# Second pass of the scores on 128 rows: keys' hi and lo parts in two copies each, in a two-layer hybrid encoder

## Chip, cores and metric

One core of a Trainium2 chip runs the whole program as one launch. The metric is the device time of one execution in microseconds (us); the median over runs is compared. The profile is of one execution, whose own time is given beside its span.

## What is computed

The reference is a two-layer encoder on 512 tokens of width 1024. Each layer projects the normalised residual stream once and feeds four token mixers in parallel:

- A: latent attention of 4 heads over all 512 keys, with a contraction of 64 + 32 = 96;
- B: attention in a band of +-128 tokens, 4 query heads of 64 on 2 key heads, with a sink per head;
- C: neighbourhood attention on an 8 x 64 grid, 4 heads of 64;
- D: three groups of dilated band attention, 4 heads of 64 each, combined by their softmax denominators.

Each mixer's output is projected, multiplied by a sigmoid gate and summed; an output projection, a LayerNorm, a squared-ReLU MLP with a gated embedding and a second LayerNorm follow. For a head of 64 the scores are

```python
s = jnp.einsum('bnqhgd,bnkhd->bnhgqk', qb, kw).astype(jnp.float32) * dh ** -0.5
```

so the contraction of a score is over 64 values only.

## The kernel before

**Numbers in two parts.** Matmul operands are split into a hi part (rounded to fp32r by an ACT copy, `acopy`, L106) and a lo part (the rest, by a DVE subtraction, `vsub`, L109). A product of two matrices is hi x hi + hi x lo + lo x hi, three passes into the same PSUM bank. For weights the 128x1024 chunk is loaded by a DMA on SP's queue (`load`, L149), its hi part is made by ACT (L106) and its lo part by POOL (L170); a GEMM tile (`gemm_T`) takes 24 matmuls of 128x512.

**Heads of 64.** The array has 128 rows and a head needs 64. `evac_q2` puts one head's hi part into 64 partitions of a slot and its lo part into the other 64, for two heads a slot each. `evac_k2` (L353) takes the PSUM tile of two key heads and makes three slots: `ka` with the hi part of the first head in both halves, `kb` with that of the second head in both halves, and `kl` with the lo part of the first head in the upper half and of the second in the lower. ACT makes two copies of 64x512 and DVE two subtractions, both from PSUM; then L365 and L366 copy each hi part to the other half, from SBUF to SBUF on DVE. `QK.scores` (L378) then needs two matmuls for a score tile: the first over all 128 rows (q hi and q lo times k hi), the second over 64 rows (q hi times k lo):

```python
P.mm(out, qv(self.q), kv(self.k), True, False)
P.mm(out, qv(self.qh), kv(self.kl), False, True)
```

`evac_k2` is called five times a layer: for B (tile `T` 2), for C (7 and 8) and for D (12 and 18). `QK.scores` is called 16 times a layer in each of B, C (in `attn_band`) and D (in `attn_D`, where four matmuls of `FD` over 64 rows follow it directly).

**Order of the work.** The program is in written order on each engine. `Prog.run` interleaves a list of main generators (GEMM tiles, cut into granules of `P.gran` matmuls) with a list of small steps (`pipeline`, L444): each step of an attention issues the scores and softmax of one unit (S), the scaling of an earlier one (N), its transposes (T) and the product with the values (V), with lags of 1, 3 and 5 steps in A and B, and 1, 5 and 7 in C and D. So TensorE gets blocks of main matmuls with attention matmuls between them. The run of stage A ends with the three tiles of B's queries and keys; the run of stage B begins with 8 matmuls of its first main tile and then the first scores of B.

**The arena.** `R` holds `N_SLOT` slots of 128x512, 16 of them the normalised stream. `Arena.alloc` takes the next run of free slots after the last one given, in a ring; `release` frees. A weight chunk takes 4 slots. `Prog.ahead` decides how far weights are split ahead of their use: up to two chunks beyond the one taken (`P.look`), one more if many slots are free, and none that isn't needed at once while free slots less 4 are below `P.least` (7 from the start of a layer to the end of its stage D, then 0).

Of the kernel before, what the change touches and what calls it, by code (L numbers as in the profile page):

```python
# [11 lines left out]
F32 = mybir.dt.float32  # L12
# [5 lines left out]
DEPTH = 2  # L18
ALPHA = float((2 * DEPTH) ** 0.25)
NEG = -1e30  # L20
N_SLOT = 64


class Arena:
    def __init__(self, n):
        self.free = [True] * n
        self.at = 0
# [18 lines left out]
class Prog:  # L46
    def __init__(self, ctx, tc, a, out):
# [13 lines left out]
        self.PS = ps.tile([128, 8, 512], F32, name="PS")  # L61
        self.R = const.tile([128, N_SLOT, 512], F32R, name="R")
        self.M = const.tile([128, 8, 512], F32, name="M")
# [11 lines left out]
        self.hh, self.hl = 0, 8  # L75
        self.ar = Arena(N_SLOT)
        for i in range(16):
# [272 lines left out]
    return sa, sb  # L350


def evac_k2(P, ps, src=None):  # L353
    nc = P.nc
    sa, sb, sl = P.ar.alloc(1), P.ar.alloc(1), P.ar.alloc(1)
    ka, kb, kl = P.R[:, sa, :], P.R[:, sb, :], P.R[:, sl, :]
    v = lambda x: x
    if src:
        ps = src(ps)
        v = lambda x: x.rearrange("p (c t) -> p c t", c=4)  # L360
    P.acopy(v(ka)[0:64], ps[0:64])
    P.acopy(v(kb)[64:128], ps[64:128])
    P.vsub(v(kl)[0:64], ps[0:64], v(ka)[0:64])
    P.vsub(v(kl)[64:128], ps[64:128], v(kb)[64:128])
    nc.vector.tensor_copy(ka[64:128], ka[0:64].bitcast(F32))  # L365
    nc.vector.tensor_copy(kb[0:64], kb[64:128].bitcast(F32))  # L366
    return sa, sb, sl


class QK:  # L370


    def __init__(self, P, q, k, kl, pos):
        self.q, self.k = P.R[:, q, :], P.R[:, k, :]
        r = slice(0, 64) if pos == 0 else slice(64, 128)
        self.qh, self.kl = P.R[r, q, :], P.R[r, kl, :]

    def scores(self, P, out, qv, kv):  # L378
        P.mm(out, qv(self.q), kv(self.k), True, False)
        P.mm(out, qv(self.qh), kv(self.kl), False, True)  # L380

# [363 lines left out]
def layer(P, l, pend):  # L747

    nc, a = P.nc, P.a
    tok = lambda c: (lambda k: P.R[:, P.hh + k, 128 * c:128 * c + 128], lambda k: P.R[:, P.hl + k, 128 * c:128 * c + 128])  # L750
    P.gb = [0, 1, 2]
    P.least, P.reserve = 7, 24


    P.look, P.extra, P.more = 0, 0, 6
# [67 lines left out]
    kv, kvw = [], []  # L823
# [117 lines left out]
    def a_end():  # L941
# [3 lines left out]
    B = {}  # L945
    P.gran = GRAN['A']
    tB = [T_tile(0, store(B, 0, lambda ps: evac_q2(P, ps, 0.125))),
          T_tile(1, store(B, 1, lambda ps: evac_q2(P, ps, 0.125))),
          T_tile(2, store(B, 'k', lambda ps: evac_k2(P, ps)))]
    steps_A = [a_first, a_second]  # L950
    for h in range(4):
# [33 lines left out]
    D = {'qk': {}}  # L985
# [39 lines left out]
    yA = Y(P)  # L1025
    P.run([gateA(j) for j in range(8)] + tB, steps_A + pre(lambda: biasB(0)) + attn_A(P, A, yA))
    qb = {0: (B[0][0], 0), 2: (B[0][1], 1), 1: (B[1][0], 0), 3: (B[1][1], 1)}
    headB = [QK(P, qb[h][0], B['k'][h // 2], B['k'][2], qb[h][1]) for h in range(4)]


    brw = {}
# [18 lines left out]
    def vC(i):  # L1050
        def evac(ps):
# [18 lines left out]
          T_tile(5, store(C, 'q0', lambda ps: evac_q2(P, ps, 0.125)), True),  # L1070
          T_tile(6, store(C, 'q1', lambda ps: evac_q2(P, ps, 0.125)), True),
          T_tile(7, store(C, 'k0', lambda ps: evac_k2(P, ps)), True),
          T_tile(8, store(C, 'k1', lambda ps: evac_k2(P, ps)), True)]
    yB = Y(P)
    stB = attn_band(P, 'B', headB, lambda h, j: vBt[:, j, h // 2].rearrange("p x d -> p (x d)"), biasB, yB,
# [13 lines left out]
    headC = []  # L1089
    for h in range(4):  # L1090
        q, k = C[f'q{h // 2}'], C[f'k{h // 2}']
        headC.append(QK(P, q[h % 2], k[h % 2], k[2], h % 2))


    def gated(n, j, y, last=False):
# [49 lines left out]

    def d_heads(p, t):
        for i in range(2):
            D['qk'][2 * p + i] = QK(P, t['q'][i], t['k'][i], t['k'][2], i)

    def d_free(t):  # L1150
        for s in [*t['q'], *t['k']]:
# [7 lines left out]
    vD_far()  # L1159
    P.run(near0 + far0)  # L1160
    d_heads(0, t0)
    P.run([gated(2, j, yC) for j in range(4)] + near1, attn_D(P, D, (0, 1), yD) + pre(lambda: bias_first(2)))
    d_free(t0)
    P.run(far1)
    d_heads(1, t1)
    P.run([gated(2, j, yC) for j in range(4, 8)], attn_D(P, D, (2, 3), yD))
    d_free(t1)
# [114 lines left out]
    for gi, (j0, j1) in enumerate(FF_GROUPS):  # L1282
        fs = []
        for j in range(j0, j1):
            w = P.take((l, 'f1', j))
            ps = P.PS[:, P.bank(), :]
# [3 lines left out]
            r = P.tmp("relu")  # L1290
# [3 lines left out]
            s = P.ar.alloc(1), P.ar.alloc(1)  # L1294
# [26 lines left out]
    for c in range(4):  # L1321
        ps = P.PS[:, P.bank(), :]
# [24 lines left out]
def hybrid_encoder(ctx: ExitStack, tc: tile.TileContext, a, out):  # L1347
# [3 lines left out]
    with tc.manual_schedule():  # L1351
# [33 lines left out]
        for l in range(DEPTH):  # L1385
            pend = layer(P, l, pend)
# [117 lines left out]
```

## Time and profile before

| | us |
|---|---|
| median of 3 runs | 1997.35 (1996.52 to 1997.78) |
| the profiled execution's own time | 1997.37 |
| its span, first to last instruction | 1995.5 |
| TensorE (PE) busy | 1954.3 |
| POOL, DVE, ACT busy | 840.3, 777.1, 755.2 |

The page gives busy time by engine, the chain of work that ended last, and groups of instructions by line. Most instructions come from helpers, so matmuls all have line L94 (transposes L97), ACT copies L106 and DVE subtractions L109; the shapes tell them apart. A matmul's row reads `rows*columns` of the weights, then `rows x columns` of the moving data. Matmul records overlap: the end of one is modelled, so the pace of TensorE is read from start to start. A weight load (PEld) is a record of its own.

### The profile page before, as it was taken

The page shows a single profiled execution, that of the slowest core. Times are in us where ns is not written, and L with a number is a line of the kernel's source. Part 1 is how long each engine was busy: PE and PEld are TensorE (multiplying, and loading weights), DVE is VectorE, ACT ScalarE, POOL GpSimd, SP SyncE. Part 2 cuts the span into 40 slices and gives each one's busy share as a digit, 9 for nine tenths or more (in the row PEclk, how much of TensorE's full clock was granted, in tenths as well). Part 3 has the DMA queues.
Part 4 walks back from the last instruction along what each step waited for, and adds up shares of the span by engine and source line. Part 5 has one row for each costly group of instructions (what it writes and reads, how often), then busy time and mean ns, then how long its engine had stood idle before and what let it go on. Part 6 is the DMA issues. An engine that isn't in the chain of part 4 may idle for free.

```text
span 1995.5 us, 24072 instructions
## 1 busy us (share of the span) xinstructions
PE 1954.3 (98%) x9440; PEld 1611.4 (81%) x9440; DVE 777.1 (39%) x1565; ACT 755.2 (38%) x1313; POOL 840.3 (42%) x407
## 2 busy tenths in 40 slices
PE   7999999999999999999999999999999999999998
PEld 6777878787888888888888788787888888888886
DVE  6665564435243202112366656625332621021125
ACT  4554544434324322313235544434333333133130
POOL 4322344433655453534532224343436545345352
PEclk9999999999999999999999999999999999999999
DMA  4312232221432232323332123232314233223232
GB/s 168 108 54 82 99 112 97 89 82 61 147 117 95 96 126 74 107 87 103 122 111 68 57 82 103 82 125 72 101 56 168 96 102 101 102 84 127 67 120 78
DMA packets 59697, 195.96 MB, mean 98 GB/s; under 512 B 6720, under 2 KB 11968, under 8 KB 59584
## 3 DMA queue, kind: packets, MB, share of 16 engines
q1 hardware_dynamic: 56256, 188.13, 28.0%
q0 software_dynamic: 1152, 4.19, 0.7%
q10 hardware_dynamic: 2176, 2.10, 0.3%
q8 instruction: 74, 1.21, 0.2%
q14 instruction: 39, 0.32, 0.1%
HBM read 186.01 MB, written 8.39 MB: 97 GB/s over the span
## 4 chain that ended last, share of the span: by engine, by line
PE 66%; DVE 3%; ACT 1%; POOL 1%; DMA 1%; issue 1%; DVEq 0%; ACTq 0%; POOLq 0%
PE PS L94 64%; PE PS L97 2%; ACT R L106 1%; POOL R L170 1%; DVE R L109 1%; DMA raw<-in_wO_dram 0%; DMA raw<-in_wPL_dram 0%; DVE gate L1254 0%; DVE FD L303 0%; DVE FD L301 0%; DVE p L394 0%; ACT p L386 0%; DVE qf L916 0%; DVE ysum L421 0%; DVE rt L915 0%
## 5 line engine op out<-in xcount | busy, mean ns | idle before, releaser
L94 PE MATMUL PS<-R 128*128 128x512 f32 (+4 forms) x8528 | 1886.2, 378 | 12.3 <-DVE R L365 5.3
L94 PEld LDWEIGHTS PS<-R 128*128 128x128 f32 (+1 forms) x8528 | 1508.5, 187 | 333.0 <-issue 37.6
L170 POOL TENSOR_TENSOR R<-raw,R 128x1024 fp32r<-128x1024 f32 (+1 forms) x304 | 734.7, 2421 | 848.5 <-ACT R L106 811.2
L106 ACT ACTIVATE R<-raw 128x1024 fp32r<-128x1024 f32 x306 | 321.1, 1053 | 340.8 <-PE PS L94 143.5
L106 ACT ACTIVATE R<-PS 128x128 fp32r<-128x128 f32 (+5 forms) x300 | 131.7, 450 | 131.9 <-PE PS L97 82.3
L109 DVE TENSOR_TENSOR R<-PS,R 128x512 fp32r<-128x512 f32 (+5 forms) x276 | 134.4, 494 | 118.7 <-ACT R L106 117.5
L1109 POOL TENSOR_TENSOR M<-M,gate 128x512 f32<-128x512 f32 x48 | 62.1, 1293 | 191.7 <-DVE gate L1108 135.5
L386 ACT ACTIVATE p<-p,s 128x256 f32<-128x256 f32 (+2 forms) x96 | 66.1, 688 | 187.1 <-DVE s L551 65.4
L1293 DVE TENSOR_TENSOR ff<-relu 128x512 f32<-128x512 f32 x64 | 44.3, 692 | 222.1 <-ACT relu L1291 222.1
L1305 DVE TENSOR_TENSOR FD<-FD,PS 128x512 f32<-128x512 f32 x40 | 27.5, 687 | 242.5 <-PE PS L94 242.5
L1291 ACT ACTIVATE relu<-PS 128x512 f32<-128x512 f32 x64 | 38.3, 599 | 168.5 <-PE PS L94 168.5
L394 DVE TENSOR_SCALAR p<-p,s 128x512 f32<-128x512 f32 (+3 forms) x128 | 95.0, 742 | 4.5
L97 PE MATMUL PS<-ident,p 128*128 128x128 f32 x480 | 73.6, 273 | 2.8 <-DVE p L394 1.7
L97 PEld LDWEIGHTS PS<-ident,p 128*128 128x128 f32 x480 | 58.6, 140 | 16.1 <-DVE p L394 2.5
L109 DVE TENSOR_TENSOR R<-ff,R 128x512 fp32r<-128x512 f32 x64 | 44.3, 692 | 47.6 <-ACT R L106 47.6
L1108 DVE SCALAR_TENSOR_TENSOR gate<-gate,PS 128x512 f32<-128x512 f32 x48 | 32.9, 686 | 71.1 <-ACT gate L1104 42.8
L106 ACT ACTIVATE R<-ff 128x512 fp32r<-128x512 f32 x64 | 40.5, 632 | 50.9 <-DVE ff L1293 50.9
L393 DVE RECIPROCAL s<-s 128x1 f32<-128x1 f32 x128 | 20.9, 163 | 79.3 <-ACT p L386 78.1
L277 POOL TENSOR_TENSOR s<-s,mhalf 128x1 f32<-128x1 f32 x18 | 21.4, 1192 | 71.9 <-DVE s L275 71.9
L627 DVE CUSTOM_DVE_ANT_0 p<-PS,bd 128x512 f32<-128x512 f32 x32 | 21.8, 682 | 76.1 <-PE PS L94 76.1
L386 ACT ACTIVATE p<-PS,s 128x512 f32<-128x512 f32 x32 | 22.0, 689 | 53.2 <-DVE s L481 53.0
L106 ACT ACTIVATE R<-M 128x512 fp32r<-128x512 f32 (+3 forms) x20 | 13.8, 695 | 62.3 <-POOL M L1109 52.7
(100 smaller groups left out, 707.6 us busy)
## 6 DMA issues: line engine op xcount, KB each, us to landing
raw<-in_wF_dram SPq DMA_DIRECT2D x128, 512.0 KB, 3.4
raw<-in_wT_dram SPq DMA_DIRECT2D x106, 512.0 KB, 3.5
raw<-in_wBR_dram SPq DMA_DIRECT2D x16, 512.0 KB, 3.5
raw<-in_wO_dram SPq DMA_DIRECT2D x16, 512.0 KB, 3.6
raw<-in_wPG_dram SPq DMA_DIRECT2D x16, 512.0 KB, 3.4
raw<-in_wVD_dram SPq DMA_DIRECT2D x12, 512.0 KB, 3.4
hsp<-FD SPq DMA_DIRECT2D x8, 512.0 KB, 6.1
FD<-hsp SPq DMA_DIRECT2D x8, 512.0 KB, 5.9
```

The costliest lines, as they stand in the source:

```text
L94: self.nc.tensor.matmul(out, l, r, start=start, stop=stop, skip_group_check=True)
L97: self.nc.tensor.transpose(out, in_, self.ident)
L106: self.nc.scalar.activation(out=out, in_=in_, func=AF.Copy, scale=scale)
L109: self.nc.vector.tensor_tensor(out=out, in0=a, in1=hi.bitcast(F32), op=ALU.subtract)
L170: nc.gpsimd.tensor_tensor(out=lo, in0=raw, in1=hi.bitcast(F32), op=ALU.subtract)
L386: P.nc.scalar.activation(out=pt[:, 0:n], in_=src, func=AF.Exp, bias=nm, scale=1.0, accum_out=den)
L394: nc.vector.tensor_scalar(out=pt[:, 0:n], in0=pt[:, 0:n], scalar1=rd, scalar2=0.5, op0=ALU.mult, op1=ALU.mult)
L1108: nc.vector.scalar_tensor_tensor(out=t, in0=t, scalar=1.0, in1=pb, op0=ALU.add, op1=ALU.mult)
L1109: nc.gpsimd.tensor_tensor(out=P.M[:, j, :], in0=P.M[:, j, :], in1=t, op=ALU.add)
L1291: nc.scalar.activation(out=r, in_=ps, func=AF.Relu)
L1293: nc.vector.tensor_tensor(out=f, in0=r, in1=r, op=ALU.mult)
L1305: nc.vector.tensor_tensor(out=u, in0=u, in1=ps, op=ALU.add)
```

## The change

`evac_k2` now allocates four slots: `k[0]` and `k[1]` hold the hi parts of the two heads, each in both halves, and `k[2]` and `k[3]` their lo parts, each in both halves. All eight halves are written from PSUM: four ACT copies, then four DVE subtractions; the two copies from SBUF to SBUF are gone. `QK` uses the whole query slot and the whole lo slot in the second pass, so that q lo x k lo is added as well. The arena has 65 slots in place of 64, and `P.least` is 4 in place of 7.

```diff
--- before.py
+++ after.py
@@ -18,7 +18,7 @@
 DEPTH = 2
 ALPHA = float((2 * DEPTH) ** 0.25)
 NEG = -1e30
-N_SLOT = 64
+N_SLOT = 65
 
 
 class Arena:
@@ -350,34 +350,29 @@
     return sa, sb
 
 
-def evac_k2(P, ps, src=None):
-    nc = P.nc
-    sa, sb, sl = P.ar.alloc(1), P.ar.alloc(1), P.ar.alloc(1)
-    ka, kb, kl = P.R[:, sa, :], P.R[:, sb, :], P.R[:, sl, :]
-    v = lambda x: x
-    if src:
-        ps = src(ps)
-        v = lambda x: x.rearrange("p (c t) -> p c t", c=4)
-    P.acopy(v(ka)[0:64], ps[0:64])
-    P.acopy(v(kb)[64:128], ps[64:128])
-    P.vsub(v(kl)[0:64], ps[0:64], v(ka)[0:64])
-    P.vsub(v(kl)[64:128], ps[64:128], v(kb)[64:128])
-    nc.vector.tensor_copy(ka[64:128], ka[0:64].bitcast(F32))
-    nc.vector.tensor_copy(kb[0:64], kb[64:128].bitcast(F32))
-    return sa, sb, sl
+def evac_k2(P, ps):
+
+    s = [P.ar.alloc(1) for _ in range(4)]
+    k = [P.R[:, x, :] for x in s]
+    top, low = slice(0, 64), slice(64, 128)
+    for x, y in ((top, low), (low, top)):
+        P.acopy(k[0][x], ps[top])
+        P.acopy(k[1][y], ps[low])
+    for x in (top, low):
+        P.vsub(k[2][x], ps[top], k[0][top])
+        P.vsub(k[3][x], ps[low], k[1][low])
+    return s
 
 
 class QK:
 
 
-    def __init__(self, P, q, k, kl, pos):
-        self.q, self.k = P.R[:, q, :], P.R[:, k, :]
-        r = slice(0, 64) if pos == 0 else slice(64, 128)
-        self.qh, self.kl = P.R[r, q, :], P.R[r, kl, :]
+    def __init__(self, P, q, k, pos):
+        self.q, self.k, self.kl = [P.R[:, s, :] for s in (q, k[pos], k[2 + pos])]
 
     def scores(self, P, out, qv, kv):
         P.mm(out, qv(self.q), kv(self.k), True, False)
-        P.mm(out, qv(self.qh), kv(self.kl), False, True)
+        P.mm(out, qv(self.q), kv(self.kl), False, True)
 
 
 
@@ -749,7 +744,7 @@
     nc, a = P.nc, P.a
     tok = lambda c: (lambda k: P.R[:, P.hh + k, 128 * c:128 * c + 128], lambda k: P.R[:, P.hl + k, 128 * c:128 * c + 128])
     P.gb = [0, 1, 2]
-    P.least, P.reserve = 7, 24
+    P.least, P.reserve = 4, 24
 
 
     P.look, P.extra, P.more = 0, 0, 6
@@ -1025,7 +1020,7 @@
     yA = Y(P)
     P.run([gateA(j) for j in range(8)] + tB, steps_A + pre(lambda: biasB(0)) + attn_A(P, A, yA))
     qb = {0: (B[0][0], 0), 2: (B[0][1], 1), 1: (B[1][0], 0), 3: (B[1][1], 1)}
-    headB = [QK(P, qb[h][0], B['k'][h // 2], B['k'][2], qb[h][1]) for h in range(4)]
+    headB = [QK(P, qb[h][0], B['k'], h // 2) for h in range(4)]
 
 
     brw = {}
@@ -1089,7 +1084,7 @@
     headC = []
     for h in range(4):
         q, k = C[f'q{h // 2}'], C[f'k{h // 2}']
-        headC.append(QK(P, q[h % 2], k[h % 2], k[2], h % 2))
+        headC.append(QK(P, q[h % 2], k, h % 2))
 
 
     def gated(n, j, y, last=False):
@@ -1145,7 +1140,7 @@
 
     def d_heads(p, t):
         for i in range(2):
-            D['qk'][2 * p + i] = QK(P, t['q'][i], t['k'][i], t['k'][2], i)
+            D['qk'][2 * p + i] = QK(P, t['q'][i], t['k'], i)
 
     def d_free(t):
         for s in [*t['q'], *t['k']]:
```

## Rows read from the trace of the kernel before

**Rows 1.** The page, busy time and share of the span by engine

```profile
PE 1954.3 (98%) x9440; PEld 1611.4 (81%) x9440; DVE 777.1 (39%) x1565; ACT 755.2 (38%) x1313; POOL 840.3 (42%) x407
```

**Rows 2.** Stretches: us, busy by engine (PE, PEld, DVE, ACT, POOL), granted clock, DMA; B, C

```profile
157.00:235.00 78.00, 76.63 (x435) 63.77 (x436) 41.65 (x133) 38.26 (x91) 21.59 (x9) 0.98 0.26 87
235.00:316.00 81.00, 81.00 (x370) 62.53 (x369) 52.13 (x117) 35.72 (x75) 35.56 (x18) 1.00 0.26 91
```

**Rows 3.** Groups by shape on PE: busy us, mean ns, idle before

```profile
L94 PE MATMUL PS<-R 128*128 128x512 f32 x6944 | 1647.4, 393 | 2.0 <-ACT vd L106 2.0
L94 PE MATMUL PS<-R 96*128 96x512 f32 x96 | 27.7, 396 | 0.8 <-DVE R L109 0.8
...
L94 PE MATMUL PS<-R 64*128 64x512 f32 x32 | 15.8, 494 | 0.0
```

**Rows 4.** Timeline of PE around one score of C: start us, us, what

```profile
262.42 0.28 PE L94 MATMUL PS<-R 128*128 128x256 f32 x1
262.62 0.38 PE L94 MATMUL PS<-R 64*128 64x256 f32 x1
262.93 0.50 PE L94 MATMUL PS<-R 128*128 128x512 f32 x1
263.27 0.40 PE L94 MATMUL PS<-R 128*128 128x512 f32 x1
```

**Rows 5.** Chain of waits and timeline of PE, plain matmuls of 512 and 256 columns

```profile
590.62 5.47 PE PS L94 x24
...
321.40 9.32 PE L94 MATMUL PS<-R 128*128 128x256 f32 x74
```

**Rows 6.** Groups by shape on PEld

```profile
L94 PEld LDWEIGHTS PS<-R 64*128 64x128 f32 x96 | 17.5, 183 | 27.0 <-issue 25.7
```

**Rows 7.** Timeline of PE around one score of D

```profile
369.84 0.39 PE L94 MATMUL PS<-R 128*128 128x512 f32 x1
370.16 0.49 PE L94 MATMUL PS<-R 64*128 64x512 f32 x1
370.50 0.60 PE L94 MATMUL PS<-FD 64*128 64x128 f32 x4
371.03 0.50 PE L94 MATMUL PS<-R 128*128 128x512 f32 x1
```

**Rows 8.** Timeline of all engines, B's key tile is taken from PSUM

```profile
152.20 1.21 ACT L106 ACTIVATE R<-PS 64x512 fp32r<-64x512 f32 x2
...
153.45 1.39 DVE L109 TENSOR_TENSOR R<-PS,R 64x512 fp32r<-64x512 f32 x2 [0.54 <-ACT R L106]
...
154.85 2.35 DVE L365 CAST R<-R 64x512 fp32r<-64x512 f32 x1
...
158.28 3.81 PE L94 MATMUL PS<-R 128*128 128x512 f32 x9
```

**Rows 9.** Waits of PE: us in total, times, longest

```profile
PE PS L94 <- DVE R L365: 5.3, 2, 2.7
...
PE PS L97 <- DVE p L394: 1.7, 2, 0.9
```

**Rows 10.** Stretches, columns as in rows 2: the clock after idle PE

```profile
158.50:161.90 3.40, 3.40 (x9) 2.63 (x8) 0.89 (x4) 1.35 (x5) 0.00 (x0) 0.50 0.47 174
...
1002.90:1004.65 1.75, 0.04 (x1) 0.00 (x0) 1.65 (x3) 0.60 (x1) 1.75 (x2) 1.00 0.00 0
1004.65:1009.00 4.35, 4.31 (x32) 4.31 (x33) 4.32 (x4) 2.31 (x4) 2.23 (x1) 1.00 0.21 59
...
1144.90:1148.30 3.40, 3.40 (x9) 2.64 (x9) 0.68 (x3) 2.02 (x5) 0.17 (x1) 0.50 0.34 131
```

**Rows 11.** The page and groups by shape: the split of a weight chunk, the copy of L365

```profile
L170 POOL TENSOR_TENSOR R<-raw,R 128x1024 fp32r<-128x1024 f32 (+1 forms) x304 | 734.7, 2421 | 848.5 <-ACT R L106 811.2
L106 ACT ACTIVATE R<-raw 128x1024 fp32r<-128x1024 f32 x306 | 321.1, 1053 | 340.8 <-PE PS L94 143.5
...
L365 DVE CAST R<-R 64x512 fp32r<-64x512 f32 x10 | 24.0, 2403 | 0.2
```

## The prediction

> **What bounds the kernel now.** I read the page first: PE is busy 98% of the span, every other engine under half [rows 1]. A busy PE can still be a slow one, so the next view is the stretches of stages B and C, where most of the touched code runs: PE is busy 76.6 of 78 us and 81.0 of 81, DVE, ACT and POOL at most 52 us [rows 2]. So time comes off only where PE's own work gets shorter, or where PE waits. Third, the groups by shape: a matmul over 64 rows takes longer in its record than one over 128, 494 ns against 393 for the same 512 columns, while one over 96 rows takes 396 [rows 3]. Fourth, because ends are modelled, I went to starts: the timeline around a score, and a plain run to compare it with [rows 4, 5]. The same loss shows from the side of the weight loads: before the 96 loads for 64 rows PEld idles 25.7 us with nothing that the profile names [rows 6]. Last come the waits of PE, of which one belongs to the touched lines: L365, 5.3 us in two waits, one a layer [rows 9].
>
> **Scores in B and C, 64 of them.** Plain pace: 24 matmuls of 512 columns in 5.47 us are 0.228 us each; 74 of mostly 256 columns in 9.32 us are about 0.125 each [rows 5]. Around a score of C, from start to start [rows 4]: the first pass takes 0.20 (262.42 to 262.62), the second over 64 rows 0.31, the next 512-column matmul 0.34: 0.85 together. At the plain pace the three would take 0.125 + 0.125 + 0.228 = 0.48. I read the excess as: TensorE finishes what is under way before it goes to 64 rows, loads those weights in the open, and does both again on the way back; the three steps are too long by 0.08, 0.19 and 0.11. With 128 rows in both passes nothing is left to switch, so the excess of 0.37 to 0.39 goes; I take 0.38. The wider scores have 384 columns; I give them the same, since the loss lies at the switch and not in the columns (the record's excess is likewise about 100 ns at 512 columns [rows 3]). B and C have 2 x 16 scores in each of 2 layers: 64 x 0.38 = **24.3 us, all on PE's path**. That 96-row matmuls show no excess [rows 3] says that a contraction short of 128 does not cost by itself.
>
> The Trainium skill, "TensorE: Matmul & The Clock Gate", section "Why this matters for your kernels", says that a lone matmul with a small contraction takes the same time as one with 128 rows. By that the second pass has nothing to give back. The trace differs: 494 against 393 ns [rows 3].
>
> **Scores in D, 32 of them: nothing.** There four 64-row matmuls of FD follow the second pass [rows 7]. Before: first pass to second 0.32 (0.09 over plain), second to FD 0.34 (0.11 over), the way back from 371.03 on. After: the second pass comes at the plain 0.23, and the switch, with the same drain and the same open load, stands in front of FD. Bounds: if the move from R to FD costs another drain of 0.09, +2.9 us; if the switch is cheaper before a 128-column matmul, by at most the open load, 32 x 0.11 = -3.5. I take 0, as the four steps are the same.
>
> **The evacuation, ten times.** ACT gets two copies more, DVE loses L365 and L366 (L365 alone is 24.0 us in all, 2.4 each [rows 11]) and gets two subtractions. From B's key tile [rows 8]: two copies take 1.21, two subtractions 1.39; so ACT +1.2 a call, DVE 2.4 less 1.4 = 1.0 shorter at the least. In C and D the work around hides this: PE waits for no evacuation there [rows 9]. Without that cover it would cost 1.2 x 8 = 10 us.
>
> **The end of stage A, twice, is not hidden.** PE has run its 8 cover matmuls and waits 2.7 us for L365 [rows 9]. DVE's first subtraction began at 153.45, just when the second of the two copies ended (153.41), though it needs only the first [rows 8]. So I expect it behind all four copies now: copies 152.20 to 154.65, subtractions 0.70 each from there. The first pass needs only the copies, so it starts at about 154.8. The second needs `k[2]` in both halves, the third subtraction: 154.65 + 2.1 = 156.75, with about 0.1 to PE 156.87. Then the first 512-column matmul starts at 157.0, the next at 157.22; that one starts at 158.28 now [rows 8]. It gains 1.06, of which 0.38 is counted above: 0.65 x 2 = **1.3 us**. Ends: all four subtractions awaited, 0; subtractions that don't wait for the later copies, 1.2 a layer more, 3.7 in all. So this is a wait that is mostly replaced, by DVE again.
>
> **The clock after that wait.** Shortly after each of the two waits the granted clock is 0.50 (1.2 GHz) for 3.4 us [rows 10], worth 1.7 us each at half pace. After another idle of 1.75 us it stays at 1.00 [rows 10]. The new wait splits into about 0.1 and about 2.0, nearer to 1.75 than to 2.7, so I take it that the clock does not fall: **3.4 us**, with 0 as the other end.
>
> **Arena, `least`, 65 slots.** A split ahead needed 11 free slots, now 8, with one slot more in all and one (B, C) to three (end of B) more taken by keys. In slots of before that is 8 to 10, always under 11: no split comes later by this rule, and near the front of each layer one chunk more is split early. That puts an ACT copy of 1.05 and a POOL subtraction of 2.42 [rows 11] into a stage where PE waits on small steps: between -1 and +1 us a layer, taken as 0. SP's loads follow the splits and move with them; the same number is issued on each queue.
>
> **Sum.** 24.3 + 1.3 + 3.4 = 29.0 us. The profiled execution's own time, 1997.37, equals the median, 1997.35. So **1968.4 us**.
>
> **Rivals.**
> 1. *B's softmax takes half of it back.* B's units (78 us by 16 is 4.9) come 0.38 closer together, and N is only one step behind S. If PE then waits for the scaling at L394, B's 32 x 0.38 = 12.2 us are gone: 1980.6. Against it: in B PE waits on no softmax now; the only such waits are 1.7 us in all, at the tail of A [rows 9]. Chance 0.07.
> 2. *Weight loads don't overlap on equal rows.* If a load could run beside a matmul only on other rows, a second pass on all 128 rows would keep its open load and so would the next: 64 x 0.22 = 14 us stay, 1982.5. The Trainium skill states such a rule, "TensorE: Matmul & The Clock Gate", section "Part 3: Packing small matmuls — row/col tiling". By that rule plain matmuls, all on equal rows, would run at 0.34 each; they run at 0.228 [rows 5], so the trace does not agree. Chance 0.02.
> 3. *The switch is not the cause* and the excess belongs to any second pass: only the 1.3 us at the end of A are left, 1996.0, no difference that shows. Against it are the 96-row matmuls of A, three passes into one bank at 396 ns [rows 3]. Chance 0.03.
> 4. *Slower, by slots.* One slot fewer is free through C. If chunks are then written into slots that PE has just read, ACT waits for PE, and a chunk comes 1.05 + 2.42 = 3.5 us late [rows 11]. It decides from 29 / 3.5 = 8 late chunks on; if all 16 gate tiles of C are late, 56 - 29 = +27, 2024. For it: C is where fewest slots are free. Against it: PE is not idle there at all, 81.0 of 81 us [rows 2], with up to two chunks ahead, 2 x 5.5 us of matmuls. Chance 0.05.
>
> **How the numbers follow.** The forecast has 0.83. A difference of 0.2%, 4 us, is about what a measurement of this kernel can tell from none. Low end: 24.3 + 3.7 + 3.4 and a little of D, 1963. High end: no gain at the wait (0), the clock falling as now (0) and D's +2.9 give 1976; to take in rivals 1 and, nearly, 2 it goes to 1981. Faster is the forecast with rivals 1 and 2: 0.92; same 0.03; slower 0.05.
>
> **What would show it.** Right: no 64-row group on R is left and the scores of B and C are 256- and 384-column matmuls at the plain pace; PEld's unexplained idle before 64-row loads of R is gone; in D the 0.09 and 0.11 stand before FD; PE's wait at the start of B is about 2 us, for L109 in place of L365; B and C are each about 6 us shorter a layer. Wrong: new waits of PE on L394 in B; waits on L170 or L106 in C; the second pass over 128 rows still 0.3 us from start to start; or a clock of 0.50 still behind the end of A, which alone makes it 3.4 us worse.

## The result and the profile after

The changed kernel takes 1967.88 us (median of 4 runs, 1966.97 to 1969.65) against 1996.93 in the runs of the kernel before beside it: a ratio of 0.9856, with a 95% interval of 0.9839 to 0.9874. The forecast was 1968.4. The profiled execution took 1968.78 us at a span of 1966.9; before it was 1997.37 at 1995.5, so the two profiles differ by the same 28.6 us.

The page of the changed kernel, busy time by engine:

```profile
PE 1927.0 (98%) x9440; PEld 1609.1 (82%) x9440; DVE 760.9 (39%) x1565; ACT 763.7 (39%) x1333; POOL 840.5 (43%) x407
```

The number of matmuls is the same as before [rows 1] and PE's busy time is 27.3 us less. PE is still busy 98% of the span: the same work, done at a better pace, not a bound that moved elsewhere.

Where the time went off shows when the same work is compared stretch by stretch. A stretch from the first transpose of C's values to the first softmax of D holds 29 of the 32 scores of B and C. The stretches of the kernel before, in layer 1 and 2 (columns as in rows 2):

```profile
168.60:366.60 198.00, 196.98 (x1037) 161.81 (x1037) 100.30 (x249) 89.60 (x184) 78.37 (x37) 1.00 0.29 99
1154.30:1352.40 198.10, 197.08 (x1037) 161.85 (x1037) 100.25 (x250) 89.27 (x184) 78.44 (x37) 1.00 0.30 99
```

and of the changed kernel:

```profile
166.10:352.60 186.50, 185.54 (x1036) 160.99 (x1034) 94.69 (x249) 91.32 (x190) 78.13 (x37) 1.00 0.32 105
1136.90:1323.50 186.60, 185.59 (x1036) 161.07 (x1035) 94.50 (x250) 91.54 (x190) 78.26 (x37) 1.00 0.32 106
```

Each is 11.5 us shorter, 0.40 us for each of the 29 scores (a little of it belongs to the way back from the score just ahead and to D's first one); idle time has not changed (about 1.0 us in each of the four). The other place is the crossing from A to B, from the last 96-row score of A to the same first transpose. Before:

```profile
140.40:168.60 28.20, 25.00 (x111) 19.18 (x110) 13.98 (x30) 12.35 (x24) 7.14 (x3) 0.94 0.21 71
1126.20:1154.30 28.10, 24.99 (x110) 19.18 (x109) 14.07 (x30) 12.46 (x24) 7.13 (x3) 0.94 0.20 69
```

After:

```profile
139.60:166.10 26.50, 23.96 (x111) 19.30 (x110) 12.48 (x30) 13.42 (x26) 7.20 (x3) 0.94 0.24 76
1112.10:1136.90 24.80, 22.35 (x111) 18.18 (x110) 12.58 (x29) 13.53 (x26) 7.18 (x3) 1.00 0.22 70
```

It holds three scores, and is 1.7 us shorter in layer 1 and 3.3 in layer 2, where the clock no longer falls. 23.0 + 1.7 + 3.3 = 28.0 of the 28.6 us lie in these stretches. Of the rest, the start of the program is 0.7 us shorter, up to the first 96-row score (80.8 against 81.6 us); in the ten profiles of this case that point lies between 80.0 and 82.3 us, so 0.7 us there says nothing about the change.

Around one score of C (timeline of PE, start and us; compare [rows 4]) the switch has gone. A narrow window shows two overlapping matmuls as one line, whose start is the first one's:

```profile
253.42 0.40 PE L94 MATMUL PS<-R 128*128 128x256 f32 x2
253.54 0.52 PE L94 MATMUL PS<-R 128*128 128x256 f32 x2
253.66 0.40 PE L94 MATMUL PS<-R 128*128 128x512 f32 x1
...
253.89 0.40 PE L94 MATMUL PS<-R 128*128 128x512 f32 x1
```

First pass to second 0.12, second to the next matmul 0.12, that one to its successor 0.23: 0.47 us in place of 0.85. In D (compare [rows 7]) the switch stands one matmul later:

```profile
361.66 0.39 PE L94 MATMUL PS<-R 128*128 128x512 f32 x1
361.97 0.71 PE L94 MATMUL PS<-FD 64*128 64x128 f32 x4
362.61 0.50 PE L94 MATMUL PS<-R 128*128 128x512 f32 x1
362.95 0.39 PE L94 MATMUL PS<-R 128*128 128x512 f32 x1
```

From the second pass, at 361.66, to FD is 0.31, over the plain 0.23; the four FD matmuls now last 0.71 by their records in place of 0.60, since the open load of weights is among them; the way back (0.34 from 362.61) is unchanged. The weight loads show the same move: the group of loads for 64 rows of R, with its 25.7 us of unexplained idle time [rows 6], is gone, and the loads for FD, whose idle time was 1.4 us, now read

```profile
L94 PEld LDWEIGHTS PS<-FD 64*128 64x128 f32 x128 | 16.5, 186 | 11.4 <-issue 7.1 <-DVE R L109 3.6 <-DVE s L388 0.7
```

The end of A in layer 1 (ACT and DVE, then PE; compare [rows 8]):

```profile
151.39 2.42 ACT L106 ACTIVATE R<-PS 64x512 fp32r<-64x512 f32 x4
...
153.84 2.81 DVE L109 TENSOR_TENSOR R<-PS,R 64x512 fp32r<-64x512 f32 x4 [1.75 <-PE PS L94]
...
155.99 1.31 PE L94 MATMUL PS<-R 128*128 128x256 f32 x5 [2.03 <-DVE R L109]
```

The four copies end at 151.39 + 2.42 = 153.81 and the first subtraction starts right there. (Its row names PE as what ended the wait; at the same place, after the same 1.75 us, the profile of experiment 5 names ACT's copies.) The third ends at 153.84 + 3 x 0.70 = 155.94, and PE's second pass starts at 155.99. The waits of PE for L109, before the change (first line) and after it (compare [rows 9]; the L365 row is gone, L389 is the L394 of before):

```profile
PE PS L94 <- DVE R L109: 3.2, 7, 0.9
...
PE PS L94 <- DVE R L109: 7.1, 9, 2.0
...
PE PS L97 <- DVE p L389: 1.8, 2, 0.9
```

Two waits, of 2.0 us each, have been added to L109, in place of 5.3 us for L365.

### The profile page after: what moved, and what is told of

Its sections match the earlier page's. It is cut to its first block, busy times and chain, and to the rows that moved or that the text cites. A ratio compares the mean times of both kernels' runs of the same rounds, so it can differ in the third digit from the quotient of the medians.

```text
span 1966.9 us, 24093 instructions
## 1 busy us (share of the span) xinstructions
PE 1927.0 (98%) x9440; PEld 1609.1 (82%) x9440; DVE 760.9 (39%) x1565; ACT 763.7 (39%) x1333; POOL 840.5 (43%) x407
## 4 chain that ended last, share of the span: by engine, by line
PE 86%; DVE 6%; ACT 4%; DMA 1%; POOL 1%; issue 1%; SPq 0%; ACTq 0%; DVEq 0%; POOLq 0%
PE PS L94 83%; PE PS L97 3%; ACT R L106 2%; DVE R L109 1%; POOL R L170 1%; DMA raw<-in_wPL_dram 1%; ACT p L381 1%; DVE FD L303 0%; DMA M<-in_wCQ_dram 0%; DMA raw<-in_wO_dram 0%; DVE p L389 0%; DVE ysum L416 0%; DVE qf L911 0%; DVE gate L1249 0%; DVE s L476 0%
## 5 line engine op out<-in xcount | busy, mean ns | idle before, releaser
L94 PE MATMUL PS<-R 128*128 128x512 f32 (+4 forms) x8528 | 1853.1, 376 | 10.7 <-DVE R L109 7.1
L109 DVE TENSOR_TENSOR R<-PS,R 128x512 fp32r<-128x512 f32 (+5 forms) x296 | 148.3, 507 | 120.2 <-ACT R L106 116.8
L106 ACT ACTIVATE R<-PS 128x128 fp32r<-128x128 f32 (+4 forms) x320 | 143.6, 459 | 122.6 <-PE PS L97 71.1
L389 DVE TENSOR_SCALAR p<-p,s 128x512 f32<-128x512 f32 (+3 forms) x128 | 97.7, 763 | 4.5
L109 DVE TENSOR_TENSOR R<-ff,R 128x512 fp32r<-128x512 f32 x64 | 44.3, 692 | 47.7 <-ACT R L106 47.7
```

The costliest lines, as they stand in the source:

```text
L94: self.nc.tensor.matmul(out, l, r, start=start, stop=stop, skip_group_check=True)
L106: self.nc.scalar.activation(out=out, in_=in_, func=AF.Copy, scale=scale)
L109: self.nc.vector.tensor_tensor(out=out, in0=a, in1=hi.bitcast(F32), op=ALU.subtract)
L389: nc.vector.tensor_scalar(out=pt[:, 0:n], in0=pt[:, 0:n], scalar1=rd, scalar2=0.5, op0=ALU.mult, op1=ALU.mult)
```

## The experiments

All times are medians beside the kernel before on the same chip, whose medians were 1998.89 us for the first four and 1998.42 for the last four.

**1. The rows alone undone.** `QK` as before, on the new slots:

```diff
-        self.q, self.k, self.kl = [P.R[:, s, :] for s in (q, k[pos], k[2 + pos])]
+        self.q, self.k = P.R[:, q, :], P.R[:, k[pos], :]
+        r = slice(0, 64) if pos == 0 else slice(64, 128)
+        self.qh, self.kl = P.R[r, q, :], P.R[r, k[2 + pos], :]
 ...
-        P.mm(out, qv(self.q), kv(self.kl), False, True)
+        P.mm(out, qv(self.qh), kv(self.kl), False, True)
```

> The changed kernel with the second pass back on 64 rows (B, C and D), everything else as changed (four slots, eight halves from PSUM, 65 slots, least 4). It leaves out q lo x k lo, as the kernel before did. Theory (the switch between 128 and 64 rows costs 0.38 us a score in B and C): 64 x 0.38 = 24 us of the gain go, 1992 us, and the 96 matmuls over 64 rows of R read about 0.1 us longer again. Rival (the gain is from the evacuation, the arena or the order): it stays near 1968.

Measured: 1989.2 us, ratio 0.9951 (0.9935 to 0.9968). The gain of the scores is gone; the stretch of 29 scores is back where it was before:

```profile
164.20:362.20 198.00, 197.04 (x1038) 161.85 (x1037) 94.90 (x250) 92.61 (x190) 78.23 (x37) 1.00 0.29 101
1145.50:1343.50 198.00, 197.04 (x1037) 161.84 (x1037) 95.12 (x250) 92.84 (x190) 78.29 (x37) 1.00 0.29 101
```

with the evacuation and the arena as in the changed kernel. So neither of these made the 11.5 us, and that rival falls. The total was 3 us better than expected, and the start of B gives a reason:

```profile
154.88 3.99 PE L94 MATMUL PS<-R 64*128 64x256 f32 x16 [0.62 <-DVE R L109]
```

PE waits 0.62 us there in place of 2.03. With the second pass on 64 rows it needs only the upper half of `k[2]`, the first subtraction and not the third: two subtractions, 1.4 us a layer. In this profile the granted clock also stays at 1.00 behind both waits, where the changed kernel's falls once (1.7 us, below); the total does not separate the two. The longer wait is a price of the 128 rows that the change pays in this one place, hidden in its total.

**2. 64 rows in D alone.**

```diff
-            D['qk'][2 * p + i] = QK(P, t['q'][i], t['k'], i)
+            D['qk'][2 * p + i] = QK(P, t['q'][i], t['k'], i, True)
```

(`True` gives the half slots of experiment 1.)

> The changed kernel with the second pass on 64 rows in D alone (q lo x k lo is left out there); B and C as changed. Theory (in D the switch only moves by one matmul, since FD's four matmuls over 64 rows follow): no difference to the changed kernel, 1968 within 1.5 us. Rival (each second pass over 64 rows costs 0.38 wherever it stands): 32 x 0.38 = 12 us more, 1980.

Measured: 1968.87 us, 0.985 (0.9835 to 0.9865), no difference to the changed kernel. The second pass of D over 128 rows gave nothing, as forecast.

**3. The evacuation head by head.**

```diff
-    for x, y in ((top, low), (low, top)):
-        P.acopy(k[0][x], ps[top])
-        P.acopy(k[1][y], ps[low])
-    for x in (top, low):
-        P.vsub(k[2][x], ps[top], k[0][top])
-        P.vsub(k[3][x], ps[low], k[1][low])
+    for i, src in ((0, top), (1, low)):
+        P.acopy(k[i][src], ps[src])
+        P.acopy(k[i][low if i == 0 else top], ps[src])
+        for x in (top, low):
+            P.vsub(k[2 + i][x], ps[src], k[i][src])
```

> The changed kernel with the evacuation of the keys written head by head: two copies and two subtractions of the first head, then of the second. Theory (the wait at the start of B is for the third subtraction, which stands behind four copies): copies and subtractions of the first head end 1.2 + 1.4 = 2.6 us after the key tile, while PE has about 2.3 us of cover, so the wait falls from 2.0 to at most 0.4 us in each layer and the clock falls in none: 3.2 to 4.0 us less, and 1.7 more against a run in which it fell once: 1963 to 1965 us. Rival (something else holds PE there): 1968, with a wait of 2 us still there.

Measured: 1963.65 us (1962.93 to 1964.54), 0.9825 (0.9811 to 0.984): 5.2 us less than experiment 2 beside it. The timeline of ACT and DVE at the end of A:

```profile
150.55 1.20 ACT L106 ACTIVATE R<-PS 64x512 fp32r<-64x512 f32 x2
...
151.78 1.38 DVE L109 TENSOR_TENSOR R<-PS,R 64x512 fp32r<-64x512 f32 x2 [0.53 <-ACT R L106]
...
153.25 1.20 ACT L106 ACTIVATE R<-PS 64x512 fp32r<-64x512 f32 x2 [1.51 <-DVE R L109]
...
154.49 1.40 DVE L109 TENSOR_TENSOR R<-PS,R 64x512 fp32r<-64x512 f32 x2 [1.33 <-ACT R L106]
```

The first head is done at 151.78 + 1.38 = 153.16, and PE's second pass starts right behind it:

```profile
153.21 0.62 PE L94 MATMUL PS<-R 128*128 128x256 f32 x2
```

PE has no idle time of over 0.1 us there in its records (the weight load of that pass waits 0.4), in place of 2.03 us, and the granted clock falls in neither layer. The two engines take turns at the tile: ACT's second pair waits 1.51 us for DVE, though all that it shares with DVE's subtractions is the PSUM tile that both read. So the order of writing decides who is served first. This version computes what the changed kernel computes and is faster.

**4. `least` 7 with 65 slots.**

```diff
-    P.least, P.reserve = 4, 24
+    P.least, P.reserve = 7, 24
```

> The changed kernel with P.least 7 again, 65 slots kept. By the rule of the arena two splits a layer, during the gate tiles 35 and 36 in C, come one chunk later; all others stay. Theory (the threshold is worth nothing, the chunks are early enough): 1968 within 1.5 us. Rival (late splits cost 3.5 us each): 4 x 3.5 = 14 us more, 1982.

Measured: 1969.41 us, 0.9852 (0.9837 to 0.9868): no difference. The threshold is worth nothing in time.

**5. The changed kernel again**, as the measure for experiments 6 to 8.

> The changed kernel itself, unaltered, as the measure for the other runs on this chip. Both theories: 1968 within 1.5 us.

Measured: 1969.25 us (1968.51 to 1971.49), 0.9858 (0.9844 to 0.9871).

**6. The 64-row matmuls of D on 128 rows, padded with zeros.**

```diff
-                    P.mm(p1[:, 128 * g:128 * g + 128], P.FD[r, g, qs], P.FD[r, 2 + g, qs], g == 0, True)
+                    P.mm(p1[:, 128 * g:128 * g + 128], D['z', h][g][:, qs], P.FD[:, 2 + g, qs], g == 0, True)
```

where `D['z', h][g]` are slots that get

```diff
+                P.acopy(q[on], by4(ps)[on], scale)
+                nc.vector.tensor_scalar(out=P.R[off, s, :], in0=ps[off], scalar1=0.0, scalar2=None, op0=ALU.mult)
```

> The changed kernel with the 64-row matmuls of D on 128 rows too: each head's queries of the far groups go to a slot of their own whose other 64 rows are zeros (two ACT copies and two DVE products with zero per tile more), against the keys of both heads. The queries of the far groups are rounded to fp32r in it. Theory (every visit to 64 rows costs about 0.39 us, whichever matmul makes it): no 64-row matmul is left in the program, 32 x 0.39 = 12.5 us less, 1955.5. Rival (the cost in D belongs to the change from R's number format to FD's and would stay, as between the value passes over R and those over FD): about 0.19 of each 0.39 stays, 6.4 us less, 1961.5.

Measured: 1962.48 us (1961.73 to 1966.67), 0.9824 (0.981 to 0.9837): 6.8 us less than experiment 5. By the total alone that is the rival's 6.4. The timeline of PE around the same score of D says otherwise:

```profile
362.33 0.39 PE L94 MATMUL PS<-R 128*128 128x512 f32 x1
362.56 0.60 PE L94 MATMUL PS<-FD,R 128*128 128x128 f32 x4
362.92 0.48 PE L94 MATMUL PS<-R 128*128 128x512 f32 x1
363.23 0.40 PE L94 MATMUL PS<-R 128*128 128x512 f32 x1
```

From the second pass to the last line shown it takes 0.90 us, against 361.66 to 362.95 = 1.29 in the changed kernel: 0.39 is gone, all of it, although FD's number format still differs. All 32 visits (a visit is one change to 64 rows and back) read the same, 1.297 us on average in the trace of experiment 5 and 0.905 here. So 32 x 0.39 = 12.5 us were taken off PE's path here too, and the rival falls. Much of it came back as waits of PE for other engines:

```profile
PE PS L97 <- DVE FD L303: 16.5, 6, 11.0
...
PE PS L97 <- DVE R L109: 4.2, 4, 1.1
```

In experiment 5 the same two rows read 13.0 and 1.1 us: 6.6 us more waiting, 3.1 at D's transposes (L109), 2.5 at the first LayerNorm of each layer, and 1.0 at the start of the program, which has nothing to do with D. The stretch from D's first FD matmul to its last, in layer 1 of experiment 5 and then of this run, shows what is left:

```profile
352.60:466.90 114.30, 114.30 (x581) 91.65 (x580) 53.71 (x147) 50.17 (x103) 43.28 (x21) 1.00 0.24 80
353.90:464.50 110.60, 109.35 (x582) 91.36 (x580) 56.21 (x150) 51.34 (x105) 43.28 (x21) 1.00 0.26 83
```

It is 3.7 us shorter, and so in layer 2; up to the first LayerNorm 1.6 and 1.2 us are lost again. By the traces 4.6 us are left of the 12.5, by the medians 6.8. The profiled execution was the longest of its five, 1966.67 us, and its clock fell after both waits at the start of B, in experiment 5 after one; so the medians may hold some 2 us that these two traces do not show. Why D's transposes and the LayerNorm became late is read from the waits only and was not tried.

**7. Keys of the far groups in R as well.** As experiment 6, with the copies of `FD` 2 and 3 written to slots.

> As d_pad, with the keys of the far groups in slots of R as well, so that all matmuls of D's scores are fp32r; queries and keys of the far groups are rounded. By the theory (rows alone cost) the same time as d_pad. By the rival (the number format costs as well) 6 us less than d_pad: 1955.5.

Measured: 1960.75 us (1957.59 to 1962.79), 0.9812 (0.9799 to 0.9825). It does not decide what it was meant to: each FD product in f32 is recorded as two matmuls, in fp32r as one, so this run also takes 64 matmuls off (9376 in place of 9440), which neither expectation counted; and PE's waits for L109 at its transposes read 9.5 us, against 4.2 in experiment 6. The question was settled by the timeline of experiment 6.

**8. Experiments 3 and 6 together.**

> by_head and d_pad together (queries of the far groups rounded). By the theory both gains add, since one lies at the start of B and the other in D: 4.5 us below d_pad, 1951 if rows alone cost, 1957 if the number format costs as well.

Measured: 1958.81 us (1957.36 to 1959.26), 0.9802 (0.9789 to 0.9816): the lowest of all, 10.4 us under experiment 5. The gains of 3 (5.2) and 6 (6.8) add but for 1.6 us. It rounds the queries of the far groups, so it is not the same computation as the changed kernel's.

## Why the prediction was right

- **Scores in B and C, 24.3 us:** measured 23.0 in the two stretches of 29 scores; with the six remaining ones at the 0.39 that one score shows, 25.3. The scores of 384 columns, which had no row of their own, gain the same: with the 512-column matmul behind them they take 0.97 us from start to start in the trace of before and 0.58 in that of after. Undoing the rows alone (1) gives back just these 11.5 us a layer; taking other matmuls off 64 rows (6) takes 0.39 off PE's path at each visit. That the cost lies in the switch is shown by D: there the same row change gave nothing (2) until the neighbours were on 128 rows too. The Trainium skill, "TensorEngine Tiling (Array Packing)", section "Key Properties", says that a change of the tiling mode drains TensorE; the traces agree, as far as the step in front of a 64-row matmul is 0.09 us longer than plain.
- **The two rules that the prediction named.** The Trainium skill, "TensorE: Matmul & The Clock Gate", section "Why this matters for your kernels", says that a lone matmul of small contraction takes the time of a full one. For the matmuls themselves the traces agree: four of FD take 0.60 us by their records over 64 rows [rows 7] and over 128 (experiment 6). But it does not give what one costs between matmuls over 128 rows: 0.38 us more here, so the longer record that the prediction held against it is the switch and not the matmul. The same page of the Trainium skill, section "Part 3: Packing small matmuls — row/col tiling", says that a load overlaps with a matmul only on other rows; the traces do not agree: second passes over 128 rows start 0.12 us after the first, with their load hidden.
- **D, nothing:** the steps came as worked out, but for the open load, which shows behind the first FD matmul and not in front of it; (2) shows no difference.
- **The wait at the start of B, 1.3 us:** the mechanism was as put, third subtraction behind four copies, 155.94 worked out from the rows and 155.99 seen. The size, from layer 2, where the clock stayed up: 3.3 us less 3 x 0.39 for its scores and 1.7 for the clock leave 0.4; in layer 1, where the clock fell again, 1.7 less 1.2 leave 0.5; against 0.65 a layer. By the rows of the waits themselves, 5.3 less 3.9 for both layers, it is 0.7 a layer. Which of the two it is hangs on what the score right at the wait gained, and is not shown.
- **The clock, 3.4 us: half of it.** This is the term that was most mis-sized. In the profiled run it fell after the first wait and not after the second, so 1.7 us came:

```profile
157.30:160.70 3.40, 3.40 (x9) 2.62 (x9) 0.74 (x4) 2.33 (x5) 0.08 (x1) 0.50 0.67 208
1128.30:1131.70 3.40, 3.31 (x15) 2.78 (x16) 2.05 (x8) 1.81 (x5) 1.30 (x1) 1.00 0.29 59
```

The step "nearer to 1.75 than to 2.7, so I take it that the clock does not fall" was too sure: in the profiles of the changed kernel and of experiments 2 and 4 to 7, which all have this wait at 1.9 to 2.0 us in both layers, the clock fell after 4 of the 12. With the wait at 0.9 in place of 1.3 the two terms were 2.1 us too much, of which the scores gave back 1.0 and the start of the program, by chance, 0.7. So the mechanisms were right, but that the sum lies within 0.5 us is in part luck.
- **Evacuation, arena, `least`:** nothing, as forecast: in (1), which has all three, the stretches of 29 scores are as long as before; PE's waits for L109 grew by the two at the start of B alone; and (4) shows it for `least`. That the 65th slot costs nothing by itself was not tried apart.
- **Rivals:** in B no wait for L389 appeared (1.8 us in all, against 1.7 before), so the first fell. Rivals 2 to 4 fell with the stretches above: plain pace, no waits in C. A loss of the first rival's kind, scores closer together and PE's transposes then waiting for DVE, did show itself in D when the gain there was forced (6), though the wait named there is for L109 and not for the scaling.

## What to carry to other kernels

Read TensorE from start to start where it looks fully busy: a matmul over 64 rows between matmuls over 128 cost 0.38 us here beyond its own time, half of it in its neighbours' steps, and a second pass on all rows, with duplicated or zero operands, takes that away. How much of it reaches the total depends on what PE meets next: all of it in B and C, between a third and little over a half in D (4.6 or 6.8 us of 12.5). Count the visits and not the matmuls, and check what stands next to each, or the switch only moves. Where two engines read one PSUM tile in turn, write first what the next consumer needs.

## What the runs showed that was not expected

- The clock after the same wait is not the same in every run: after 2.03 us of idle PE it fell to 0.50 in the profiled run of the changed kernel, and after the same 2.03 us in the same place it stayed at 1.00 in that of experiment 2:

```profile
153.40:155.40 2.00, 0.00 (x0) 0.00 (x1) 1.94 (x4) 0.77 (x1) 1.15 (x1) 1.00 0.00 0
157.00:160.40 3.40, 3.40 (x17) 2.86 (x16) 1.24 (x5) 2.22 (x5) 1.03 (x1) 1.00 0.61 212
```

In experiment 6 it fell after both, here in layer 2, after 1.95 us:

```profile
1128.20:1131.60 3.40, 3.40 (x9) 2.65 (x9) 1.15 (x6) 1.74 (x5) 0.33 (x1) 0.50 0.53 177
```

With 1.7 us for each fall and two such places, runs of one kernel may differ by up to 3.4 us by this alone (an estimate). It fits that experiment 3, without the waits, has the narrowest runs of the first four, 1962.93 to 1964.54, against 1966.66 to 1970.69 in experiment 4.
- ACT and DVE do not read one PSUM tile side by side in this program, even where both only read: DVE's first subtraction starts 0.03 us after the last of the four queued copies ends, though it needs only the first, and ACT's second pair in experiment 3, on partitions 64 to 127, waits 1.51 us for DVE on partitions 0 to 63. Whether the chip asks for this or only the order that the program's semaphores set is not shown.
